# A three-block transformer forward pass with a product-key expert layer: gathering inside the routing, alternating expert tiles, one-hot rows in batches

## The chip, the cores and the metric

The kernel runs on one core of one Trainium2 chip as one program. The metric is the time of one execution on the device, in microseconds (us). The engines are named as in the profile: PE (TensorE, matrix products), PEld (its weight loads), DVE (VectorE), ACT (ScalarE), POOL (GpSimd) and SP (SyncE, which here only issues transfers).

## What is computed

Two blocks of a small model on 512 tokens of width 1024: two layers with feed-forward, attention, mLSTM and RWKV mixing; then one layer with a gated delta rule, an LRU and cross-attention, and last an expert layer and a norm. The change touches only the expert layer:

```
q = (t @ wq).reshape(ntok, 8, 2, 128)            # 8 heads, two half queries
sc = einsum('thpd,hpkd->thpk', q, subkeys)       # 128 keys for each half
s1, i1 = top_k(sc[:, :, 0], 16);  s2, i2 = top_k(sc[:, :, 1], 16)
best, pos = top_k(s1[..., :, None] + s2[..., None, :], 16)
idx = e1 * 128 + e2                              # one of 16384 experts
gate = softmax(best)                             # 128 (expert, gate) pairs for each token
act = gelu(einsum('phkd,pd->phk', u_tab[idx], t)) * gate
out = einsum('phk,phkd->pd', act, v_tab[idx])
```

## The kernel before, in words

Everything lies feature-major in tiles of 128 partitions. A float32 product is made of three products of split operands (high by high, high by low, low by high). A weight tile of 128 x 1024 is therefore loaded into a staging buffer `st` (two of them, 512 KB each), cast by ACT to its high part and subtracted to its low part: `load_w` (lines 173 to 183), with `wh` and `wl` for the tables of u, and lines 1809 to 1812, with `vh` and `vl`, for the tables of v.

The expert layer (`peer`, lines 1557 to 1599) treats the 512 tokens in two ways. For the first 128 tokens (one block) rows are gathered: for each of 128 slots an indirect transfer brings, for every token, the row of its own expert from the u table (`urow`, 512 KB), DVE multiplies and adds it up against the token (line 1767, one number per token into `za`), and eight slots later the row of the v table (`vrow`) is accumulated into `acc` (line 1778). For the other 384 tokens all 16384 experts are computed, 128 tiles of 128 experts: 24 products give z (`peer_z`), then gelu, then the gate of each expert and token (mostly zero), and 18 products add the tile to six accumulators in PSUM (`values`).

The stages in order:

- `peer_route`, lines 1630 to 1723: 16 tiles of query weights; for each tile `lists` (top 16 of 128 keys, for four blocks of tokens, on DVE) and for each of 8 heads `head`: candidates on POOL (`cd`), their top 16 on DVE, comparison on DVE (line 1696), product on POOL (line 1697), sum on DVE (line 1698), softmax. After each head three result tiles of the expert stage are computed early (`early`) and put into DRAM.
- `peer_gates`, lines 1725 to 1747: for each of the 384 tokens three one-hot rows of 128 (lines 1737 to 1739: `o1` the first key, `p1` and `p2` the second key times the gate's high and low part); two products give the token's 128 x 128 gate matrix; ACT copies four tokens at a time into `st` (`gst`), and 32 tokens at a time go to DRAM (`G`, 2 MB). Early result tiles, 30 of them, run between, with the subtraction of `load_w` on POOL (`wl_eng`).
- `peer_experts`, lines 1782 to 1857: 128 tiles. A tile below `NEARLY` (56) fetches its z from DRAM, the others compute it here. Each takes its gates from DRAM (`gt`, 12 pieces for four tiles), makes its activations (`ah`, `al`), loads its v tile, and the products of the tile before it follow.

The gather advances with `gather(n)`: a step of slot s is one DVE product of a u row, one DVE accumulation of a v row, and the issue of the next rows by POOL into the buffers that have come free (three for each table). Before, it begins after the routing: 12 steps in the gates, and the rest with the tiles. The order of instructions on each engine is not the source's: a scheduler places them by dependences and its own estimate, and each engine then works its queue in that order.

Of the kernel before, what the change touches and what calls it, by code (L numbers as in the profile page):

```python
# [21 lines left out]
P = 128  # L22
# [89 lines left out]
class K:  # L112
# [1444 lines left out]
    def peer(self, out):  # L1557
        nc, tc, d = self.nc, self.tc, self.d
        with ExitStack() as ctx:
# [7 lines left out]
            ez = [self.drm.tile([P, TD], F32, tag=f"z{i}", name=f"z{i}", bufs=1) for i in range(NEARLY)]  # L1567
# [7 lines left out]
            self.fin = pool.tile([P, D], F32, name="fin")  # L1575

            def early(n):
                for i in range(self.zi, min(self.zi + n, NEARLY)):
# [4 lines left out]
                    self.zi = i + 1  # L1583

            sl = [pool.tile([P, TD], F32, name=f"slot{i}") for i in range(4)]
# [6 lines left out]
            self.rowp = ctx.enter_context(tc.tile_pool(name="row", bufs=1, reuse_waits="tile"))  # L1592
# [3 lines left out]
            early(NEARLY)  # L1596
            self.wl_eng = nc.vector
# [11 lines left out]
    def token_major(self, yk):  # L1609
# [18 lines left out]
        nc.sync.dma_start(out=self.fin, in_=d["FG"])  # L1628

    def peer_route(self, pool, iota, slots, early, yk):  # L1630
# [27 lines left out]
        def lists(m, q):  # L1658
# [8 lines left out]
            if m % 2:  # L1667
                early(3)

        def head(h):  # L1670
# [39 lines left out]
        nc.vector.scalar_tensor_tensor(self.idx, tok[1][:, 0, :], float(P), tok[0][:, 0, :], op0=ALU.mult, op1=ALU.add)  # L1710
        nc.gpsimd.tensor_copy(out=self.gate0, in_=tok[2][:, 0, :])
        for w in range(3):
# [4 lines left out]
            if w < 2:  # L1717
                nc.scalar.copy(out=slots[w], in_=pf)
            else:
                hi = pool.tile([P, TD], F16, name="hi16")  # L1720
                nc.scalar.activation(hi, pf, AF.Copy, scale=GS)
                nc.vector.scalar_tensor_tensor(slots[3], pf, GS, hi, op0=ALU.mult, op1=ALU.subtract)
                nc.scalar.copy(out=slots[2], in_=hi)

    def peer_gates(self, pool, im, slots, early):

        nc = self.nc
        self.gather_begin()
        for i in range(TD // GT):
            st = pool.tile([P, P, GT], F32, tag="gst", name="gst", bufs=2)  # L1730
            for t0 in range(0, GT, 4):
                pg = self.ps([P, 4, P], "g")
                for j in range(4):
                    t = i * GT + t0 + j
                    o1, p1, p2 = (pool.tile([P, P], F16, tag=n, name=n, bufs=8) for n in ("o1", "p1", "p2"))
                    s = [x[:, t:t + 1] for x in slots]
# [6 lines left out]
                if t0 % 16 == 12:  # L1743
                    early(1)
# [261 lines left out]
```

## Time and profile before

| | us |
|---|---|
| median of 3 runs | 4692.69 (4678.49 to 4698.35) |
| profiled execution | 4696.09 |
| its span | 4694.3 |

| engine | busy us | share of the span | instructions |
|---|---|---|---|
| PE | 4337.1 | 92% | 21867 |
| PEld | 3549.2 | 76% | 21867 |
| DVE | 2823.5 | 60% | 5950 |
| ACT | 1624.7 | 35% | 2583 |
| POOL | 993.5 | 21% | 850 |

The span is from the first to the last instruction on the core. Busy shares are means over stages with different limits, so they say little on one stage. In the rows below, a group of instructions names line, engine, operation, output and inputs (partitions x elements, type) and count; then busy time and the mean of one in ns; then the engine's idle time just before them and what ended most of it. A table of windows gives the busy time of each engine in a stretch of the span, in us from its start.

### The profile page before, as it was taken

The numbers are of one execution on the slowest core, as the hardware profiler recorded it, in microseconds if no ns is written. First come the engines' busy times: TensorE is split into PE (matmuls) and PEld (weight loads), VectorE is DVE, ScalarE is ACT, GpSimd is POOL, SyncE is SP. The second block draws the span as 40 slices with busy tenths as digits, with TensorE's granted clock in tenths as the row PEclk, the third lists the DMA queues.
The fourth block names the chain that finished last, engine by engine and source line by source line (L and its number), as shares of the span: only waits on it lengthen the run. The fifth ranks groups of instructions, "written<-read, shape, count | busy, mean of one in ns | idle before, by whom it ended". The sixth has DMA issues, their size and how long they took to land. (4 is left out here: it accounts for less than half of the span.)

```text
span 4694.3 us, 58390 instructions
## 1 busy us (share of the span) xinstructions
PE 4337.1 (92%) x21867; PEld 3549.2 (76%) x21867; DVE 2823.5 (60%) x5950; ACT 1624.7 (35%) x2583; POOL 993.5 (21%) x850
## 2 busy tenths in 40 slices
PE   8999999999999989999998898998787688888998
PEld 7887787888888867878887677887654466777887
DVE  4435654542654266554427666378899888787334
ACT  3223423322532243233225434332344333322332
POOL 0002110000100031110003321023431666565111
PEclk9999998999999999889998999999997799999999
DMA  3233102323332320122233114333454889898443
GB/s 121 95 96 116 35 19 68 108 94 95 128 109 91 111 89 25 37 72 101 95 110 129 50 37 139 109 138 104 155 183 177 289 313 344 314 331 292 154 149 110
DMA packets 232300, 625.66 MB, mean 133 GB/s; under 512 B 26544, under 2 KB 91184, under 8 KB 227664
## 3 DMA queue, kind: packets, MB, share of 16 engines
q1 hardware_dynamic: 192704, 460.96, 28.8%
q0 software_dynamic: 38736, 159.93, 9.3%
q8 instruction: 171, 2.80, 0.2%
q10 hardware_dynamic: 576, 1.05, 0.1%
q14 instruction: 113, 0.93, 0.1%
HBM read 560.49 MB, written 61.34 MB: 132 GB/s over the span
## 5 line engine op out<-in xcount | busy, mean ns | idle before, releaser
L191 PE MATMUL ps_ps<-xh,wl 128*128 128x512 f32 (+2 forms) x3568 | 1327.3, 373 | 33.0 <-DVE wl L182 32.9
L191 PE MATMUL ps_ps<-xl,wh 128*128 128x512 f32 (+2 forms) x3568 | 1333.9, 374 | 24.1 <-DVE xl L338 23.4
L191 PE MATMUL ps_ps<-xh,wh 128*128 128x512 f32 (+2 forms) x3568 | 1326.8, 373 | 28.3 <-ACT wh L181 15.6
L181 ACT CAST wh<-st 128x1024 fp32r<-128x1024 f32 (+1 forms) x560 | 580.3, 1037 | 1615.7 <-PE ps_ps L191 958.1
L182 DVE TENSOR_TENSOR wl<-st,wh 128x1024 fp32r<-128x1024 f32 (+1 forms) x506 | 613.2, 1213 | 665.5 <-ACT wh L181 664.4
L191 PEld LDWEIGHTS ps_ps<-xh,wl 128*128 128x128 f32 x3568 | 689.5, 193 | 139.7 <-DVE wl L182 40.5
L191 PEld LDWEIGHTS ps_ps<-xl,wh 128*128 128x128 f32 x3568 | 689.5, 193 | 127.3 <-DVE xl L338 34.3
L191 PEld LDWEIGHTS ps_ps<-xh,wh 128*128 128x128 f32 x3568 | 686.4, 193 | 130.1 <-ACT wh L181 17.5
L343 POOL TENSOR_TENSOR y<-y,x 128x256 f32<-128x256 f32 x64 | 54.7, 855 | 1768.8 <-DVE y L342 1534.0
L437 DVE TENSOR_TENSOR gu<-ps_ps,R 128x512 f32<-128x512 f32 x176 | 121.0, 691 | 473.3 <-PE ps_ps L191 473.3
L191 PE MATMUL ps_po<-vh,ah 128*128 128x512 f32 x768 | 318.7, 415 | 66.9 <-ACT ah L1805 65.5
L191 PE MATMUL ps_po<-vl,ah 128*128 128x512 f32 x768 | 319.2, 416 | 45.5 <-DVE vl L1812 45.5
L191 PE MATMUL ps_ps<-mh,wl 128*128 128x512 f32 (+1 forms) x920 | 327.8, 356 | 2.4 <-DVE wl L182 2.4
L191 PE MATMUL ps_po<-vh,al 128*128 128x512 f32 x768 | 318.6, 415 | 11.0 <-DVE al L1806 10.3
L191 PE MATMUL ps_ps<-mh,wh 128*128 128x512 f32 (+1 forms) x920 | 327.4, 356 | 1.2 <-DVE kf L1497 0.9
L191 PE MATMUL ps_ps<-ml,wh 128*128 128x512 f32 (+1 forms) x792 | 289.4, 365 | 0.0
L191 PEld LDWEIGHTS ps_po<-vh,ah 128*128 128x128 f32 x768 | 154.0, 201 | 105.6 <-ACT ah L1805 70.9
L1802 POOL TENSOR_TENSOR z<-z,gt 128x384 f32<-128x384 f32 x128 | 155.6, 1222 | 337.2 <-ACT z L1800 307.3
L191 PE MATMUL ps_g<-p,o 128*128 128x128 f16 x768 | 173.2, 242 | 56.1 <-DVE p L1738 28.1
L191 PEld LDWEIGHTS ps_po<-vl,ah 128*128 128x128 f32 x768 | 153.9, 200 | 87.2 <-DVE vl L1812 56.7
L191 PEld LDWEIGHTS ps_po<-vh,al 128*128 128x128 f32 x768 | 153.8, 200 | 58.2 <-DVE al L1806 26.4
L191 PEld LDWEIGHTS ps_ps<-mh,wl 128*128 128x128 f32 x920 | 174.8, 190 | 26.3 <-DVE wl L182 2.7
(695 smaller groups left out, 6762.7 us busy)
## 6 DMA issues: line engine op xcount, KB each, us to landing
st<-in_pu_dram SPq DMA_DIRECT2D x128, 512.0 KB, 4.4
st<-in_pv_dram SPq DMA_DIRECT2D x128, 512.0 KB, 4.8
st<-in_w1i_dram SPq DMA_DIRECT2D x88, 512.0 KB, 3.5
st<-in_w2i_dram SPq DMA_DIRECT2D x88, 512.0 KB, 3.4
G<-gst POOLq DMA_DIRECT2D x12, 2048.0 KB, 7.7
gt<-G SPq DMA_DIRECT2D x384, 64.0 KB, 5.0
st<-in_wmf_dram SPq DMA_DIRECT2D x44, 512.0 KB, 3.5
xd<-y SPq DMA_DIRECT2D x20, 1024.0 KB, 3.8
```

Of the source, the lines that this page charges most:

```text
L181: nc.scalar.copy(out=wh[:, :n], in_=st[:, :n])
L182: self.wl_eng.tensor_sub(wl[:, :n], st[:, :n], wh[:, :n].bitcast(F32))
L191: i = self.nc.tensor.matmul(out, lhsT=lhsT, rhs=rhs, start=start, stop=stop)
L343: nc.gpsimd.tensor_add(y[k + 1], y[k + 1], self.xin[k + 1][:, c])
L437: nc.vector.tensor_mul(t, psum, R)
L1802: nc.gpsimd.tensor_mul(x3, x3, gts["g"][:, :, i % GK, :])
```

## The change

The gather begins after the first head of the routing, and takes two steps after each head, one after each 16 tokens in the gates (24), and one in three of four turns of the expert tiles (96). Its buffers are fixed: two tiles of the layer's pool and four halves of the buffers that held the layer's input. The early result tiles are no longer the first 56 but two of each four (64), and the turns of four tiles run 0, 2, 1, 3, so early and late tiles alternate. The one-hot rows are built for 16 tokens at once, with tensor-by-tensor instructions of 2048 16-bit elements, in pairs of tokens (the slots are now 16-bit, and the keys are stored twice over). The subtraction of `load_w` in the gates is on DVE again.

```diff
...
-            ez = [self.drm.tile([P, TD], F32, tag=f"z{i}", name=f"z{i}", bufs=1) for i in range(NEARLY)]
+            ez = {i: self.drm.tile([P, TD], F32, tag=f"z{i}", name=f"z{i}", bufs=1) for i in EARLY}
...
+            self.buf = [pool.tile([P, D], F32, name=f"row{i}") for i in range(2)]
...
-            im = pool.tile([P, P], F16, name="im")
-            nc.gpsimd.tensor_copy(out=im, in_=iota)
+            im = pool.tile([P, P, 2], F16, name="im")
+            nc.gpsimd.tensor_copy(out=im, in_=bc(iota.unsqueeze(2), [P, P, 2]))
...
-            self.wl_eng = nc.gpsimd
...
+        h = [self.half(F32, "rows").rearrange("p a b -> p (a b)") for _ in range(2)]
+        self.buf += [h[0][:, :D], h[0][:, D:], h[1][:, :D], h[1][:, D:]]
...
             if m % 2:
                 early(3)
+                self.gather(2)
...
+            nc.vector.scalar_tensor_tensor(self.idx[:, hs], tok[1][:, 0, hs], float(P), tok[0][:, 0, hs], op0=ALU.mult, op1=ALU.add)
+            nc.gpsimd.tensor_copy(out=self.gate0[:, hs], in_=tok[2][:, 0, hs])
+            if h == 0:
+                self.gather_begin()
...
-                    o1, p1, p2 = (pool.tile([P, P], F16, tag=n, name=n, bufs=8) for n in ("o1", "p1", "p2"))
-                    s = [x[:, t:t + 1] for x in slots]
-                    nc.vector.tensor_scalar(o1, im, s[0], None, op0=ALU.is_equal)
-                    nc.vector.tensor_scalar(p1, im, s[1], s[2], op0=ALU.is_equal, op1=ALU.mult)
-                    nc.vector.tensor_scalar(p2, im, s[1], s[3], op0=ALU.is_equal, op1=ALU.mult)
...
+            for t0 in range(0, GT, 2 * B):
+                c = slice(i * GT + t0, i * GT + t0 + 2 * B)
+                o1, p1, p2 = (pool.tile([P, B, P, 2], F16, tag=n, name=n, bufs=2) for n in ("o1", "p1", "p2"))
+                row = lambda x: bc(x[:, c].rearrange("p (a b) -> p a b", b=2).unsqueeze(2), [P, B, P, 2])
+                keys = bc(im.unsqueeze(1), [P, B, P, 2])
+                nc.vector.tensor_tensor(o1, keys, row(slots[0]), op=ALU.is_equal)
+                nc.vector.tensor_tensor(p2, keys, row(slots[1]), op=ALU.is_equal)
+                nc.vector.tensor_mul(p1, p2, row(slots[2]))
+                nc.vector.tensor_mul(p2, p2, row(slots[3]))
+                for q in range(0, B, 2):
...
+                        o, a, b = (x[:, q + j // 2, :, j % 2] for x in (o1, p1, p2))
...
+                    if q == 2:
+                        early(1)
+                early(1 if t0 else 0)
+                self.gather(1)
...
-            t = self.rowp.tile([P, D], F32, tag=w + "row", name=w + "row", bufs=3)
+            t = self.buf[s % 3 + 3 * (w == "v")]
...
-            if i < NEARLY:
+            if i in ez:
...
-            nxt = act(n)
-            due = n // 2 if n < NEARLY else NEARLY // 2 + (n - NEARLY) * 3 // 2
-            self.gather(max(0, due + TD // GT - self.gi))
+            nxt = act(n // 4 * 4 + (0, 2, 1, 3)[n % 4])
+            self.gather(n % 4 != 1)
...
-NEARLY = 56
+EARLY = [i for i in range(P) if i % 4 < 2]
...
```

POOL's queue in the routing of the changed kernel, from the end of the first head (`eq`) to the candidates of the second (`cd`); `row` and `rows` are the gather's buffers, filled from the table of u (`pur`) or of v (`pv`).

```order
L1709 COPY gate_23310<-tok_23335 128x16
L1698 TENSOR_TENSOR eq<-eq,sf 128x1024 x2
L1764 DMA row_23316<-in_pur_dram,idx 128x1024
L1764 DMA row_23317<-in_pur_dram,idx 128x1024
L1764 DMA rows<-in_pur_dram,idx 128x1024
L1764 DMA rows<-in_pv_dram,idx 128x1024
L1764 DMA row_23316<-in_pur_dram,idx 128x1024
L1764 DMA row_23317<-in_pur_dram,idx 128x1024
L1695 CAST sf<-si 128x64
L1764 DMA rows<-in_pv_dram,idx 128x1024 x2
L1678 TENSOR_TENSOR cd<-sv 128x4x8
L1675 COPY cd<-sv 128x4x128
```

Before, `eq` is followed at once by `sf` and the three steps on `cd`; now eight issues of rows stand between, and the second `row_23316` waits for the buffer of the first.

DVE's queue in the gates, before: one token.

```order
L1737 TENSOR_SCALAR o_26202<-im,slot_23308 128x128
L1738 TENSOR_SCALAR p_26203<-im,slot_23309,slot_23310 128x128
L1739 TENSOR_SCALAR p_26204<-im,slot_23309,slot_23311 128x128
L1737 TENSOR_SCALAR o_26212<-im,slot_23308 128x128
L1738 TENSOR_SCALAR p_26213<-im,slot_23309,slot_23310 128x128
```

And of the changed kernel, where this is a batch of 16 tokens:

```order
L1737 TENSOR_TENSOR o_26455<-im,slot_23318 128x2048
L1738 TENSOR_TENSOR p_26457<-im,slot_23319 128x2048
L182 TENSOR_TENSOR wl<-st,wh 128x1024
L1739 TENSOR_TENSOR p_26456<-p_26457,slot_23320 128x2048
L1774 ISA row_23317,za<-row_23317,htok 128x1024
L1774 ISA za 128x1
L1740 TENSOR_TENSOR p_26457<-p_26457,slot_23321 128x2048
L1785 SCALAR_TENSOR_TENSOR acc<-rows,za,acc 128x1024
```

The 48 instructions of 16 tokens became four, and between them stand the subtraction that was POOL's (three for 32 tokens) and a step of the gather for each batch.

DVE's queue in the expert tiles of the changed kernel; `vl` closes a loaded value tile, `wl` a weight tile of a late tile, `z` and `al` are a tile's activations.

```order
L1819 TENSOR_TENSOR vl<-st,vh 128x1024
L1774 ISA row_23316,za<-row_23316,htok 128x1024
L1774 ISA za 128x1
L1785 SCALAR_TENSOR_TENSOR acc<-rows,za,acc 128x1024
L1813 TENSOR_TENSOR al<-z,ah 128x384
L1819 TENSOR_TENSOR vl<-st,vh 128x1024
L1774 ISA row_23317,za<-row_23317,htok 128x1024
L1774 ISA za 128x1
L182 TENSOR_TENSOR wl<-st,wh 128x1024
L1806 TENSOR_TENSOR z<-ps_ps,R 128x384
L1785 SCALAR_TENSOR_TENSOR acc<-rows,za,acc 128x1024
L1774 ISA rows,za<-rows,htok 128x1024
```

Before, early tiles (a `vl` with about one step of the gather) all come first and late ones (`vl` and `wl` with two steps) after them; now each pair of tiles has two `vl`, one `wl` and three steps, and the last step stands after 59 of the 128 tiles, where it stood after 89.

## Rows read from the trace of the kernel before

**Rows 1.** Windows by stage: us, busy PE, PEld, DVE, ACT, POOL, clock, DMA, GB/s

```profile
3095.00:3349.00 254.00, 215.00 (x1090) 193.27 (x1089) 207.00 (x875) 61.55 (x91) 95.23 (x101) 0.95 0.34 114
3349.00:3662.00 313.00, 254.24 (x1476) 155.77 (x1474) 312.85 (x1184) 141.97 (x158) 92.25 (x60) 0.86 0.51 184
3662.00:3686.00 24.00, 0.00 (x0) 0.00 (x0) 19.52 (x24) 7.71 (x15) 21.68 (x13) 0.50 0.88 312
3686.00:4334.00 648.00, 550.78 (x2331) 452.08 (x2332) 535.96 (x643) 201.85 (x299) 415.46 (x311) 0.92 0.90 321
4334.00:4677.00 343.00, 339.05 (x1689) 304.75 (x1688) 136.17 (x175) 116.73 (x159) 41.91 (x41) 1.00 0.43 140
```

**Rows 2.** Groups by line and form, routing, 3095 to 3349 us

```profile
L1698 DVE TENSOR_REDUCE tok<-eq 128x64 f32<-128x1024 f32 x16 | 19.5, 1220 | 27.2 <-POOL eq L1697 27.2
L1696 DVE TENSOR_TENSOR eq<-k,iota 128x1024 f32<-128x1024 f32 x16 | 18.8, 1215 | 0.0
```

**Rows 3.** Groups by line and form, tiles with gather, 3686 to 4334 us

```profile
L1778 DVE SCALAR_TENSOR_TENSOR acc<-vrow,za,acc 128x1024 f32<-128x1024 f32 x119 | 165.4, 1390 | 8.8 <-DMA vrow<-in_pv_dram,idx 8.7
...
L1767 DVE CUSTOM_DVE_ANT_0 urow<-urow,htok 128x1024 f32<-128x1024 f32 x112 | 146.9, 1312 | 1.0 <-DMA urow<-in_pur_dram,idx 1.0
...
L1812 DVE TENSOR_TENSOR vl<-st,vh 128x1024 fp32r<-128x1024 f32 x87 | 108.3, 1245 | 9.2 <-ACT vh L1811 9.1
...
L1811 ACT CAST vh<-st 128x1024 fp32r<-128x1024 f32 x86 | 90.1, 1048 | 120.3 <-DMA st<-in_pv_dram 108.8 <-DVE acc L1778 4.5 <-DVE al L1806 4.1
...
L182 DVE TENSOR_TENSOR wl<-st,wh 128x1024 fp32r<-128x1024 f32 x34 | 41.7, 1226 | 62.4 <-ACT wh L181 62.3
```

**Rows 4.** One tile, urow, 3095 to 3662 us: ns min/median/max

```profile
L1758 POOL DMA_INDIRECT urow<-in_pur_dram,idx x15: 937/997/3129, 3348.5 to 3661.6; - x15
L1767 DVE CUSTOM_DVE_ANT_0 urow<-urow,htok x12: 1206/1214/1225, 3375.6 to 3659.0; 128x1024 f32<-128x1024 f32 x12
...
DMA to landing us min/median/max: 4.9/8.4/11.1
```

**Rows 5.** Timeline of DVE in the gates: start us, us, instruction

```profile
3589.86 0.25 DVE L1737 TENSOR_SCALAR o<-im,slot 128x128 f16<-128x128 f16 x1
...
3590.47 0.25 DVE L1737 TENSOR_SCALAR o<-im,slot 128x128 f16<-128x128 f16 x1
```

**Rows 6.** One tile, im: ns min/median/max, first and last start

```profile
L1737 DVE TENSOR_SCALAR o<-im,slot x384: 235/245/3076, 3349.6 to 3658.3; 128x128 f16<-128x128 f16 x192
```

**Rows 7.** Groups by line and form, gates, 3349 to 3662 us

```profile
L182 POOL TENSOR_TENSOR wl<-st,wh 128x1024 fp32r<-128x1024 f32 x27 | 66.0, 2444 | 109.5 <-ACT wh L181 95.1 <-PE ps_ps L191 11.5 <-PE ps_g L191 2.9
```

**Rows 8.** Groups by line and form, ramp, 3662 to 3686 us

```profile
L1799 DVE TENSOR_TENSOR z<-z,R 128x384 f32<-128x384 f32 x9 | 4.6, 551 | 0.0
```

**Rows 9.** Timeline of PE, tiles alone: first values product, first z product, next values

```profile
4401.79 0.40 PE L191 MATMUL ps_po<-vh,ah 128*128 128x512 f32 x1
...
4405.89 0.34 PE L191 MATMUL ps_ps<-xh,wh 128*128 128x384 f32 x1
...
4410.10 0.40 PE L191 MATMUL ps_po<-vh,ah 128*128 128x512 f32 x1
```

**Rows 10.** Timeline of PE in the gates: gate products, one z product between

```profile
3402.20 0.23 PE L191 MATMUL ps_g<-p,o 128*128 128x128 f16 x1
...
3402.49 0.23 PE L191 MATMUL ps_g<-p,o 128*128 128x128 f16 x1
```

**Rows 11.** DMA issues: count, KB each, median us from issue to landing

```profile
st<-in_pu_dram SPq DMA_DIRECT2D x128, 512.0 KB, 4.4
...
G<-gst POOLq DMA_DIRECT2D x12, 2048.0 KB, 7.7
gt<-G SPq DMA_DIRECT2D x384, 64.0 KB, 5.0
```

**Rows 12.** Windows inside the tiles with gather, columns as in rows 1

```profile
3800.00:3900.00 100.00, 79.18 (x296) 60.96 (x296) 81.86 (x96) 34.22 (x55) 65.71 (x48) 0.88 0.88 310
3900.00:3980.00 80.00, 71.34 (x290) 55.59 (x289) 70.72 (x89) 27.31 (x41) 51.70 (x39) 0.96 0.97 350
```

More of the change, by code (lines that the diff above doesn't have):

```diff
@@ L1575, in peer @@
             self.fin = pool.tile([P, D], F32, name="fin")
+            self.buf = [pool.tile([P, D], F32, name=f"row{i}") for i in range(2)]
             def early(n):
-                for i in range(self.zi, min(self.zi + n, NEARLY)):
+                for i in EARLY[self.zi:self.zi + n]:
                     z = self.peer_z(i)
@@ L1582, in early @@
                     nc.sync.dma_start(out=ez[i], in_=t)
-                    self.zi = i + 1
-            sl = [pool.tile([P, TD], F32, name=f"slot{i}") for i in range(4)]
+                    self.zi += 1
+            sl = [pool.tile([P, TD], F16, name=f"slot{i}") for i in range(4)]
             iota = pool.tile([P, P], F32, name="iota")
             nc.sync.dma_start(out=iota, in_=d["IOTA"])
-            im = pool.tile([P, P], F16, name="im")
-            nc.gpsimd.tensor_copy(out=im, in_=iota)
+            im = pool.tile([P, P, 2], F16, name="im")
+            nc.gpsimd.tensor_copy(out=im, in_=bc(iota.unsqueeze(2), [P, P, 2]))
             with tc.tile_pool(name="pr", bufs=1) as rp:
                 self.peer_route(rp, iota, sl, early, yk)
-            self.rowp = ctx.enter_context(tc.tile_pool(name="row", bufs=1, reuse_waits="tile"))
-            self.wl_eng = nc.gpsimd
             with tc.tile_pool(name="pg", bufs=1, reuse_waits="tile") as gp:
                 self.peer_gates(gp, im, sl, early)
-            early(NEARLY)
-            self.wl_eng = nc.vector
+            early(P)
             with tc.tile_pool(name="px", bufs=1, reuse_waits="tile") as xp:
@@ L1719, in peer_route @@
             else:
[L1720 to L1723, printed above, removed]
+                nc.scalar.activation(slots[2], pf, AF.Copy, scale=GS)
+                nc.vector.scalar_tensor_tensor(slots[3], pf, GS, slots[2], op0=ALU.mult, op1=ALU.subtract)
     def peer_gates(self, pool, im, slots, early):
@@ L1727, in peer_gates @@
         nc = self.nc
[L1728 removed]
+        B = 8
         for i in range(TD // GT):
             st = pool.tile([P, P, GT], F32, tag="gst", name="gst", bufs=2)
[L1731 to L1734, printed above, removed]
[L1735 to L1744 removed]
+            for t0 in range(0, GT, 2 * B):
[8 more added lines that the diff above has]
+                for q in range(0, B, 2):
+                    pg = self.ps([P, 4, P], "g")
+                    for j in range(4):
+                        o, a, b = (x[:, q + j // 2, :, j % 2] for x in (o1, p1, p2))
+                        self.mm(pg[:, j, :], o, a, True, False)
+                        self.mm(pg[:, j, :], o, b, False, True)
+                    t = t0 + 2 * q
+                    nc.scalar.activation(st[:, :, t:t + 4].rearrange("p k t -> p t k"), pg, AF.Copy, scale=1.0 / GS)
+                    if q == 2:
+                        early(1)
+                early(1 if t0 else 0)
+                self.gather(1)
@@ L1745, in peer_gates @@
             nc.gpsimd.dma_start(out=self.gd_[i], in_=st)
-            early(1)
-            self.gather(1)
     def gather_begin(self):
@@ L1842, in peer_experts @@
         self.gather(P + GG)
-        h = [self.half(F32, "xt").rearrange("p a b -> p (a b)") for _ in range(2)]
-        xt = [h[0][:, :D], h[0][:, D:], h[1][:, :D]]
-        sq = h[1][:, D:]
+        xt, sq = self.buf[:NB - 1], self.buf[NB]
         for b in range(NB - 1):
```

5 lines of the change are left out of this document (removed).

## Prediction

> **What bounds the kernel now.** I read the table of windows first, because a change that touches only the last third has to be priced stage by stage. [Rows 1] cut that third at its seams: the routing (254 us), the gates (313), a ramp (24) in which TensorE does nothing, a stage in which expert tiles and the gather share the core (648), and a stage with expert tiles alone (343). The 3095 us ahead are not touched. Three different things bound these stages. In the gates VectorE is busy 312.85 of 313 us, with DMA at half. In the shared stage no engine is full (TensorE 551 of 648), but DMA is at 0.90 and moves 321 GB/s. In the stage of tiles alone TensorE is busy 339 of 343.
>
> Then the groups of instructions by line. The routing has VectorE busy for 207 of 254 us [rows 1], and 27.2 of the idle 47 are the wait of a reduction for GpSimd's product [rows 2]: a chain that goes to and fro between the two. In the shared stage ScalarE's cast, which opens each loaded value tile, stood idle for 108.8 us until the load had come [rows 3]: transfers end last there, not VectorE.
>
> **The change, part by part.** The order of instructions says how many pieces lie in each stage; every duration is from a row.
>
> *Routing, +30.* Of the gather, 17 row products and 9 accumulations now stand on VectorE's queue ahead of the first one-hot row, where none stood. By 1.21 us a product [rows 4] and 1.39 an accumulation [rows 3] that is 33 us; some 2 more for index steps made head by head and for the first row, which lands after about 8.4 us [rows 4] while some ten list steps run. Only one of the 26 stands in the wait of 27.2, so I count 5 us as absorbed by other waits. Bounds: 0, if all falls into the idle 47, and 42, if nothing does and the first row is waited for whole. GpSimd gets some 30 row issues of 1.0 us [rows 4] and has 159 us idle there; ScalarE gets four more table loads and has 192 idle [rows 1]. Both hidden: nothing charged. The wait that the change adds is GpSimd's: a row is issued only when its buffer is free, and the router's casts and products are queued behind it. The cover is three buffers for each table; without it, see the last rival.
>
> *Gates, -49.* A token costs VectorE 0.61 us, start to start [rows 5], so 234 for 384; the rest of the 313 is 16 gather steps and, mostly, waiting: the equality instruction has a median of 245 ns and a maximum of 3076 [rows 6], beside 27 subtractions of 2.44 us on GpSimd [rows 7]. These go to VectorE, and that waiting goes with them. After, 32 tokens take VectorE 8 batches, 3 subtractions (1.23, [rows 3]) and 4 gather steps (1.3). No row shows a batch of 2048 16-bit numbers. By the number of elements, two float32 rows of 384 and 1024 (551 ns, [rows 8]; 1215, [rows 2]) give 1.04 ns an element, so 2.28 us. By bytes, a batch is as long as the row of 1215 ns: 1.22. The 16-bit row of today is the nearest: 128 elements would be 285 ns on the line through those two, and it takes 235 to 245 [rows 6], so it does not pay by elements. I take 1.22 and keep 2.28 as the other end. VectorE then needs 9.8 + 3.7 + 5.2 = 18.7 us for 32 tokens. TensorE needs 3 tiles of 4.21 [rows 9] and 64 gate products of 0.115 (a pair with an expert product repeats every 0.29, [rows 10], of which the latter alone is 4.21/24 = 0.175): 20.0. DMA moves one block of 2 MB, 3 weight tiles and 4 rows of 512 KB [rows 11] and 3 results of 192 KB: 6.4 MB, 19.8 us at 321 GB/s. Three resources within 7% of each other, all with queues in order, wait by turns; I add a tenth: 22 us, times 12 = 264. Bounds: 224 (12 times 18.7) and 325 (12 times 27.1, with 2.28). TensorE has expert tiles to the end of this stage, 36 of them; today they run out, and the granted clock of the stage is 0.86 [rows 1].
>
> *Ramp, 0.* The last block is written and read back (7.7 and 5.0 us, [rows 11]) before the first tile can be used. Four tiles of TensorE work now stand there; they shorten nothing of that path.
>
> *Shared stage, -168.* In VectorE's order the gather, spread over 96 of 128 turns in the source, still runs ahead: from the first cast value tile to the last accumulation there are 58 value tiles, 29 weight tiles, 85 products and 93 accumulations. Today's rows have 87, 34, 112 and 119 [rows 3]. In MB today: 121 tiles and 231 rows of 0.524, and some 140 small ones (gates and early results) of 0.197: 212, which fits [rows 1]'s 321 GB/s over 648 us. After: 87, 178 and 87 of them: 156 MB, 486 us at that rate; by loaded tiles, at 648/121 = 5.36 each, 466. I take 480. Bounds: 446 at the 350 GB/s of the best stretch [rows 12], and 557 at 280, should alternate tiles use DMA worse. For a pair of tiles, early and late, DMA needs 5.3 MB, 16.5 us; VectorE 11.8 for casts, subtractions and gather [rows 3] and some 2.4 for four small steps; TensorE 12.4 (two times 4.10, one of 4.21, [rows 9]). So DMA still ends last, and to alternate is by itself worth nothing: the gain is 53 rows and 34 tiles fewer in this stage.
>
> *Stage of tiles alone, +110.* What leaves the shared stage comes here. Today 39 value and 38 result tiles stand behind the last accumulation, 320 us by [rows 9], and it measures 343, since TensorE runs some tiles behind VectorE. After: 69 and 35, 430, with the same lag 453. TensorE is full here and stays so.
>
> *End and queues, 0.* The final normalisation takes other buffers and the same steps. The sync queue stores and fetches eight more results, 1.6 MB each way, and their bytes are inside the counts above.
>
> Sum: 30 - 49 - 168 + 110 = -77 on the profiled execution's 4696.1 (span 4694.3), which lies 3.4 above the median of the three runs shown. I forecast **4618**.
>
> **Rivals.**
> *All covers hold* (0.15). The router takes most of its 26 steps into its waits (+10), the gates come to 19 us for 32 tokens (228), and the shared stage runs at 350 GB/s (446): 10 - 85 - 202 + 110 = -167, so 4529. For it: DMA held 0.97 for 80 us [rows 12]. Against: the gates need three resources full at once.
> *The batches run one element at a time* (0.17). The slots' operand repeats one pair of 16-bit numbers for each of 128 keys; if that takes the short price away, VectorE needs 27.1 us for 32 tokens, the gates 325: 30 + 12 - 168 + 110 = -16, so 4680. For it: nothing in the trace reads this way. Against: today's 16-bit row. The Trainium skill (Vector Engine (DVE) Microarchitecture Reference, 5.2 Measured stream behaviour on trn2) says that a port keeps its full rate only for runs of two or more adjacent 4-byte words, and gives 1.73 ns a column where one source jumps at each; a pair of 16-bit numbers is one such word, so by it a batch would be an estimated 1.9 us, the gates 290 and the sum some 26 us above mine. No row of this trace can tell.
> *Transfers get worse by turns* (0.08). At 280 GB/s the shared stage is 557: 30 - 49 - 91 + 110 = 0, so 4696, no change. For it: the 100 us ahead of today's best stretch ran at 310 [rows 12]. Against: the rows for each loaded tile hardly move (231/121 = 1.91, then 178/87 = 2.05).
> *The rows hold the router* (0.05; slower). If each of the 26 steps waits as long as a row takes to land (8.4 us, [rows 4]), the routing grows by 218: 218 - 49 - 58 = 111, so 4807. It decides from 4.1 us a step (107/26). For it: VectorE and GpSimd run in order, and the router's lists, candidates and products stand behind. Against: rows are issued two or three ahead, and a head lasts 32 us (254/8).
>
> **How the numbers follow.** The forecast has 0.55 and by itself reaches from 4575 to 4660. Two in ten may stay outside: the slower rival, half of the best case, and edges of the others; so 4520 to 4690. A measurement of this kernel tells about 0.5% from no change, which puts the bounds at 4669 and 4716. Faster: of the forecast 0.54, the best case 0.15, a third of the one-element case 0.06, a little of the worse transfers 0.01: 0.76. Slower: the last rival and edges of two others, 0.08. Same: the rest, 0.16.
>
> **What would show it.** Routing: about 285 us, rows' products between the list steps, no long wait of VectorE for a row. Gates: batches of 1.2 us, 250 to 275 us in all, DMA from 0.5 to over 0.85, clock above 0.95. Shared stage: about 480 us with DMA at 0.9, and ScalarE's casts still idle for loads. Tiles alone: about 450 us, TensorE full. I am wrong if a batch takes 2 us, if the shared stage falls under 450 or stays over 540, or if GpSimd's row issues stand in front of the router's products for long.

## The result, and the profile after

The changed kernel takes **4581.2 us** (median of 4 runs, 4575.1 to 4587.6), beside 4695.5 us for the kernel before in the same session (median of 4). The ratio is 0.9758, 95% interval 0.9721 to 0.9796: 114 us faster. The forecast was 4618, 77 us faster, with a range of 4520 to 4690.

First the table of windows of the changed kernel, cut at the seams of [rows 1]: routing, gates, ramp, shared stage, tiles alone. Columns as there.

```profile
3095.00:3389.00 294.00, 239.20 (x1172) 214.43 (x1171) 242.43 (x953) 76.48 (x110) 143.14 (x136) 0.89 0.47 156
3389.00:3624.00 235.00, 211.37 (x1624) 192.02 (x1623) 204.75 (x205) 141.00 (x169) 85.08 (x58) 0.97 0.84 307
3624.00:3653.00 29.00, 12.69 (x54) 11.19 (x52) 20.31 (x23) 6.89 (x11) 13.57 (x12) 0.70 0.99 355
3653.00:4128.00 475.00, 404.46 (x1712) 334.50 (x1713) 394.23 (x465) 148.02 (x213) 319.76 (x227) 0.90 0.91 324
4128.00:4568.00 440.00, 434.92 (x2092) 380.68 (x2091) 204.73 (x256) 176.80 (x240) 81.64 (x69) 1.00 0.51 166
```

What binds each stage is what bound it before, except in the gates, where VectorE has gone from 312.85 of 313 us to 204.75 of 235 and DMA from 0.51 to 0.84; now nothing is full there, and TensorE is the busiest with 211.37. The stages follow exactly from five events in each trace: the product that makes the gathered tokens' input (`htok`), the first one-hot instruction, the last issue of a gate block, the first value product, the last accumulation of a row.

| us | before | after | difference | forecast |
|---|---|---|---|---|
| routing (`htok` to first one-hot) | 260.4 | 291.1 | +30.7 | +30 |
| gates (to last gate block) | 311.2 | 234.3 | -76.9 | -49 |
| ramp (to first value product) | 25.3 | 29.4 | +4.1 | 0 |
| shared stage (to last accumulation) | 648.3 | 474.7 | -173.6 | -168 |
| tiles alone, and the end | 359.9 | 457.3 | +97.4 | +110 |
| all of it | 1605.1 | 1486.8 | -118.3 | -77 |

The code ahead of `htok` is the same in both and took 9.4 us longer in this execution; with it the spans (4694.3 and 4585.4) differ by 108.9.

Next the groups by line and form in the routing of the changed kernel; the first answers to [rows 2].

```profile
L1699 DVE TENSOR_REDUCE tok<-eq 128x64 f32<-128x1024 f32 x16 | 19.5, 1220 | 28.4 <-POOL eq L1698 28.4
...
L1774 DVE CUSTOM_DVE_ANT_0 row<-row,htok 128x1024 f32<-128x1024 f32 x12 | 14.5, 1210 | 3.5 <-DMA row<-in_pur_dram,idx 3.5
...
L1785 DVE SCALAR_TENSOR_TENSOR acc<-rows,za,acc 128x1024 f32<-128x1024 f32 x9 | 11.6, 1291 | 0.0
...
L1774 DVE CUSTOM_DVE_ANT_0 rows<-rows,htok 128x1024 f32<-128x1024 f32 x5 | 6.2, 1239 | 0.0
```

The wait of the reduction for GpSimd is there as before (27.2, now 28.4): the rows did not fill it. VectorE waited 3.5 us in all for a row. The 17 products and 9 accumulations are those that the prediction counted.

Then the gates, same view: the gate products, the subtraction that came back to VectorE, ScalarE's cast, and a batch.

```profile
L191 PE MATMUL ps_g<-p,o 128*128 128x128 f16 x768 | 57.6, 222 | 10.1 <-DVE p L1739 8.1 <-ACT gst L1748 1.8
...
L182 DVE TENSOR_TENSOR wl<-st,wh 128x1024 fp32r<-128x1024 f32 x35 | 42.8, 1223 | 18.0 <-ACT wh L181 18.0
L181 ACT CAST wh<-st 128x1024 fp32r<-128x1024 f32 x34 | 36.1, 1062 | 82.1 <-DMA st<-in_pu_dram 82.1
...
L1737 DVE TENSOR_TENSOR o<-im,slot 128x2048 f16<-128x2048 f16 x24 | 29.3, 1222 | 0.0
```

And the shared stage, which answers to [rows 3].

```profile
L191 PE MATMUL ps_po<-vh,ah 128*128 128x512 f32 x347 | 153.8, 443 | 75.3 <-ACT ah L1812 75.2
...
L1785 DVE SCALAR_TENSOR_TENSOR acc<-rows,za,acc 128x1024 f32<-128x1024 f32 x89 | 120.5, 1354 | 4.9 <-DMA rows<-in_pv_dram,idx 4.8
...
L1774 DVE CUSTOM_DVE_ANT_0 row<-row,htok 128x1024 f32<-128x1024 f32 x55 | 71.1, 1292 | 0.1
L1818 ACT CAST vh<-st 128x1024 fp32r<-128x1024 f32 x57 | 59.7, 1047 | 35.5 <-DMA st<-in_pv_dram 17.4 <-PE ps_po L191 15.4 <-DMA gt<-G 2.7
L1774 DVE CUSTOM_DVE_ANT_0 rows<-rows,htok 128x1024 f32<-128x1024 f32 x27 | 53.9, 1995 | 0.0
...
L181 ACT CAST wh<-st 128x1024 fp32r<-128x1024 f32 x29 | 30.4, 1050 | 92.1 <-DMA st<-in_pu_dram 92.1
```

55 and 27 products and 89 accumulations where 85 and 93 were counted: the loads and rows of this stage are those of the order, and the rate is 324 GB/s where 321 was used. The cast of value tiles waits 17.4 us for loads, 108.8 in [rows 3]; that wait now stands before the cast of weight tiles, 92.1 us in this stage.

### The profile page after: what moved, and what is told of

Read it like the earlier page. It is cut to its first block, busy times and chain, and to the rows that moved or that the text cites. A ratio compares the mean times of both kernels' runs of the same rounds, so it can differ in the third digit from the quotient of the medians.

```text
span 4585.4 us, 57113 instructions
## 1 busy us (share of the span) xinstructions
PE 4281.3 (93%) x21867; PEld 3575.4 (78%) x21867; DVE 2674.0 (58%) x4931; ACT 1636.7 (36%) x2594; POOL 970.0 (21%) x827
## 5 line engine op out<-in xcount | busy, mean ns | idle before, releaser
L191 PE MATMUL ps_ps<-xh,wh 128*128 128x512 f32 (+2 forms) x3568 | 1325.2, 373 | 31.5 <-ACT wh L181 18.7
L182 DVE TENSOR_TENSOR wl<-st,wh 128x1024 fp32r<-128x1024 f32 (+1 forms) x536 | 650.8, 1215 | 539.2 <-ACT wh L181 538.0
L191 PE MATMUL ps_ps<-ml,wh 128*128 128x512 f32 (+1 forms) x792 | 289.5, 366 | 0.0
L1764 POOL DMA_INDIRECT rows<-in_pv_dram,idx x128 | 197.8, 1546 | 60.6 <-DVE acc L1785 31.3
L191 PEld LDWEIGHTS ps_ps<-mh,wh 128*128 128x128 f32 x920 | 174.5, 190 | 25.8 <-DVE kf L1497 1.2
```

What stands on the lines that cost most here:

```text
L182: self.wl_eng.tensor_sub(wl[:, :n], st[:, :n], wh[:, :n].bitcast(F32))
L191: i = self.nc.tensor.matmul(out, lhsT=lhsT, rhs=rhs, start=start, stop=stop)
L1764: self.nc.gpsimd.indirect_dma_start(out=t, out_offset=None, in_=self.d["pur" if w == "u" else "pvr"], in_offset=bass.IndirectOffsetOnAxis( ...
```

## Experiments

Every time is a median of 4 to 8 runs, with its ratio to the kernel before on the same chip; stages are from the one profiled execution of each, by the five events above. "Experts" is the shared stage and the rest together, from the first value product to the end. The changed kernel has 932.0 us there, the one before 1008.2. The part ahead of `htok`, which is the same in all of them, ends between 3084 and 3106 us in these traces, so a difference of some 20 us between two totals is to be read together with the stages.

| kernel | us | ratio, 95% interval | routing | gates | shared | rest | experts |
|---|---|---|---|---|---|---|---|
| changed | 4581.2 | 0.9758 (0.9721 to 0.9796) | 291.1 | 234.3 | 474.7 | 457.3 | 932.0 |
| rows per token again | 4666.3 | 0.9934 (0.9910 to 0.9958) | 291.0 | 329.0 | 476.8 | 445.7 | 922.5 |
| batches without pairs | 4651.2 | 0.9901 (0.9869 to 0.9932) | 290.8 | 309.5 | 475.0 | 453.7 | 928.7 |
| batches alone | 4621.5 | 0.9830 (0.9801 to 0.9860) | 261.4 | 232.0 | 583.5 | 428.9 | 1012.4 |
| early tiles first | 4606.4 | 0.9812 (0.9779 to 0.9844) | 290.1 | 234.2 | 524.8 | 433.6 | 958.4 |
| gather called after routing | 4545.2 | 0.9680 (0.9660 to 0.9700) | 273.4 | 219.9 | 516.0 | 408.1 | 924.1 |
| gather spread | 4563.7 | 0.9714 (0.9683 to 0.9745) | 289.6 | 239.3 | 889.0 | 26.9 | 915.9 |
| spread, 4 buffers | 4682.0 | 0.9970 (0.9950 to 0.9990) | 289.6 | 235.9 | 993.8 | 36.9 | 1030.7 |
| spread, z fetched | 4655.5 | 0.9904 (0.9868 to 0.9940) | 289.5 | 235.6 | 978.3 | 28.2 | 1006.5 |
| spread, both | 4614.0 | 0.9830 (0.9795 to 0.9864) | 290.2 | 235.3 | 932.4 | 37.0 | 969.4 |
| spread, two turns | 4527.9 | 0.9629 (0.9600 to 0.9658) | 291.1 | 233.1 | 853.3 | 26.9 | 880.2 |
| spread, two turns, z fetched | 4590.9 | 0.9762 (0.9746 to 0.9779) | 289.4 | 235.1 | 912.0 | 26.9 | 938.9 |
| two turns, gather called after routing | **4512.0** | 0.9601 (0.9579 to 0.9623) | 273.7 | 213.9 | 875.0 | 28.2 | 903.2 |

### The gates

Theory: the batches are what shortens the gates, and a batch takes 1.22 us because its slot operand steps through a pair of 16-bit numbers. Rival: the other parts of the change do as much.

**Rows per token again**, all else as changed.

```diff
-                nc.vector.tensor_tensor(o1, keys, row(slots[0]), op=ALU.is_equal)
...
+                    nc.vector.tensor_scalar(o1, im, s[0], None, op0=ALU.is_equal)
+                    nc.vector.tensor_scalar(p1, im, s[1], s[2], op0=ALU.is_equal, op1=ALU.mult)
+                    nc.vector.tensor_scalar(p2, im, s[1], s[3], op0=ALU.is_equal, op1=ALU.mult)
```

> The changed kernel with one part undone: the one-hot rows are again three instructions for each token; the subtraction of the weight tiles stays on VectorE, the gather stays where the change put it. Theory (VectorE's instructions made the gates long): 32 tokens cost 19.5 + 3.7 + 4.9 = 28.1 us on VectorE, so the gates go from 234 to about 335 us and the whole from 4581 to about 4680, ratio to before 0.995 to 1.0. Rival (it was the wait for GpSimd's subtractions that made them long, and the batches add little): gates 240 to 265 us, the whole 4585 to 4610.

**Batches without pairs**: the same 96 instructions of 2048 elements, with the keys innermost, so that the slot operand repeats one 16-bit number 128 times.

```diff
-                row = lambda x: bc(x[:, c].rearrange("p (a b) -> p a b", b=2).unsqueeze(2), [P, B, P, 2])
+                row = lambda x: bc(x[:, c].unsqueeze(2), [P, 2 * B, P])
```

> The changed kernel with batches of 16 tokens, but tokens not in pairs: the keys run innermost, and the slot's operand repeats one 16-bit number for 128 elements. Theory (the pair in the innermost place is what lets the batch run at the price by bytes): a batch takes about 2.28 us in place of 1.22, VectorE needs 27 us for 32 tokens, the gates come to 320 us and the whole to about 4670. Rival (16 bits suffice): 1.22 us, gates 234, 4575 to 4590.

**Batches alone**: the kernel before with the batches; beside them only the buffers of the v rows move, to make room.

```diff
+                nc.vector.tensor_tensor(o1, keys, row(slots[0]), op=ALU.is_equal)
+                nc.vector.tensor_tensor(p2, keys, row(slots[1]), op=ALU.is_equal)
+                nc.vector.tensor_mul(p1, p2, row(slots[2]))
+                nc.vector.tensor_mul(p2, p2, row(slots[3]))
...
-            t = self.rowp.tile([P, D], F32, tag=w + "row", name=w + "row", bufs=3)
+            t = self.rowp.tile([P, D], F32, tag=w + "row", name=w + "row", bufs=3) if w == "u" else self.vbuf[s % 3]
```

> The kernel before with the one-hot rows in batches of 16 tokens and nothing else of the change: early tiles stay the first 56, the gather begins in the gates, the subtraction of load_w in the gates stays on POOL (only the rows of v move to the buffers that held the layer's input, since the batches need the room). Theory: the batches alone pay the gain in the gates, and a shorter gates stage is worth its whole length because nothing after it depends on the other parts. VectorE then has 96 x 1.22 = 117 us of one-hots and some 65 us of rows in this stage, TensorE 27 tiles x 4.2 + 58 us of gate products = 171 us, so about 205 to 240 us in place of 311, and a total of 4590 to 4630, ratio 0.977 to 0.986: more than three quarters of the whole gain of 114. Rival: the parts need each other (the batches without the gather begun in the routing leave the same rows for the experts, and POOL's subtraction holds the early tiles): the gates stay over 270 us and the total over 4655.

The windows of the gates of the three, in this order, then the batch without pairs and the row products of batches alone by line:

```profile
3385.00:3714.00 329.00, 262.19 (x1588) 218.73 (x1587) 326.07 (x1259) 145.39 (x167) 57.28 (x55) 0.82 0.61 215
```

```profile
3380.00:3689.00 309.00, 226.08 (x1591) 207.95 (x1590) 304.77 (x203) 140.19 (x168) 110.66 (x57) 0.86 0.68 231
```

```profile
3357.00:3590.00 233.00, 187.39 (x1467) 178.89 (x1465) 227.05 (x181) 134.94 (x162) 172.12 (x90) 0.91 0.85 311
```

```profile
L1737 DVE TENSOR_TENSOR o<-im,slot 128x2048 f16<-128x2048 f16 x24 | 54.8, 2282 | 0.0
```

```profile
L1772 DVE CUSTOM_DVE_ANT_0 urow<-urow,htok 128x1024 f32<-128x1024 f32 x27 | 36.1, 1335 | 1.0 <-DMA urow<-in_pur_dram,idx 1.0
```

With rows per token, or with batches of 2.28 us, VectorE is full again (326 of 329, 305 of 309) and the gates are 95 and 75 us longer; the experts hardly move (922.5, 928.7). So the batch's price carries the stage, and about nine tenths of it reach the total: 85 of 95 us, 70 of 75. Batches alone give 78 us, about 70% of the gain where over three quarters were expected. They do not need the rest of the change: the scheduler put 27 row products into their gates, where 12 stood before, and GpSimd's subtractions, which stay in that run, did not hold them. The theories hold in kind; the gates of the first two are 6 and 10 us under what was expected, the totals 14 and 19.

### The order of the early tiles

The prediction has it that alternating tiles is by itself worth nothing.

```diff
-            nxt = act(n // 4 * 4 + (0, 2, 1, 3)[n % 4])
+            nxt = act(n)
...
-EARLY = [i for i in range(P) if i % 4 < 2]
+EARLY = list(range(64))
```

> The changed kernel with the alternation undone: the 64 early tiles are the first 64 and come first. In VectorE's order the gather then ends at tile 80 of 128 and not at 59. Theory (bytes at 324 GB/s): the shared stage holds 172 MB, about 530 us (475 with alternation), the stage after it about 420 (457 with the end): +20 to +40, the whole 4600 to 4620. Rival 1 (the order of early and late is worth nothing): 4570 to 4592. Rival 2 (alternation is what made the gain): over 4650.

4606, inside what was expected: **alternating is worth 25 us** by the medians, 26 in the experts. The two intervals of the ratio touch, but no run of one kernel lies among the other's. The windows of the shared stage and of the tiles alone:

```profile
3646.00:4170.00 524.00, 436.32 (x1779) 350.73 (x1779) 435.89 (x513) 172.81 (x263) 328.71 (x248) 0.91 0.90 321
4170.00:4589.00 419.00, 414.50 (x2060) 371.54 (x2059) 168.31 (x212) 141.40 (x192) 49.67 (x49) 1.00 0.44 139
```

DMA moves the same 321 GB/s. But with early tiles first, TensorE is left without work for 524 - 436 = 88 us of the shared stage; alternating, for 475 - 404 = 71: 17 of the 25 us. The shared stage also holds more, 168 MB where alternating holds 154 (rate times length, from these rows and those of the changed kernel). The prediction looked at DMA, which ends last in either order, and not at how much of TensorE's work is done meanwhile.

### The gather in the routing

With the rows in it the routing is 30.7 us longer. Do they bring as much later?

```diff
-                self.gather(2)
...
-            if h == 0:
-                self.gather_begin()
...
+        self.gather_begin()
         B = 8
...
-            self.gather(n % 4 != 1)
+            self.gather(n % 8 != 1)
```

> The changed kernel with the gather begun in the gates again: no row is fetched or worked on in the routing, and the experts take seven steps in eight turns in place of three in four. Theory (the prediction's: a step moved out of the full shared stage pays its transfer there and costs what it holds up in the routing): the routing goes from 291 back to some 260 us; 16 steps or 16 MB more in the shared stage are 16 MB / 0.32 = 50 us, and that stage ends some 8 tiles later, which takes as many from the stage of tiles alone; the sum is nearly nothing, total 4565 to 4600. Rival: the routing's 30 us are the price of POOL's queue, and what is bought with them is hidden anyway: 4550 to 4560. Other rival: the rows in the routing are what lets the shared stage end early, and without them 4610 or more.

4545: 36 us **faster** than the change, and better than the expectations. They were also wrong in one point: the scheduler still put rows into the routing, where nothing but its own estimate asked for them, 11 products and 2 accumulations in place of 17 and 9.

```profile
L1772 DVE CUSTOM_DVE_ANT_0 row<-row,htok 128x1024 f32<-128x1024 f32 x8 | 9.7, 1211 | 0.0
...
L1772 DVE CUSTOM_DVE_ANT_0 rows<-rows,htok 128x1024 f32<-128x1024 f32 x3 | 3.6, 1208 | 0.0
...
L1783 DVE SCALAR_TENSOR_TENSOR acc<-rows,za,acc 128x1024 f32<-128x1024 f32 x2 | 2.5, 1253 | 0.0
```

The routing is 17.7 shorter for 13 instructions less, 1.4 each, and the gates 14.4. The rows come back in the shared stage, which is 41.3 us longer, and the stage after it is 49.2 shorter. So as it stands in this change, a row taken in the routing costs its full time there and buys nothing: the experts take 932 us with the rows moved ahead and 924 without, though the routing and the gates then hold 11 products and 10 accumulations fewer. What a variant with no row at all in the routing would do wasn't tried.

### The gather spread over all tiles

In the shared stage TensorE is short of work, in the next one DMA. Theory: let the gather steps keep pace with the tiles (each step behind the subtraction `vl` of its turn, on VectorE), and neither is.

```diff
+                self.behind(i, self.after)
...
-            nc.vector.tensor_sub(vl, st, vh.bitcast(F32))
+            self.after = nc.vector.tensor_sub(vl, st, vh.bitcast(F32))
```

> The changed kernel with one addition: in the expert tiles each step of the gather stands behind the subtraction of its own turn's value tile on VectorE's queue (an order, no wait), so the 96 steps are spread over all 128 tiles as the source has them, and don't run ahead. Theory (DMA ends last in the shared stage and TensorE in the one after it, since the gather is bunched): a pair of tiles then needs 3.7 MB, 11.5 us at 324 GB/s, under TensorE's 12.4, so the whole expert part runs near TensorE: 64 pairs in 800 to 840 us where it now takes 915; the whole 4480 to 4520. Rival (loads are late at any mean load, for their latency with two staging buffers): the casts' idle time for loads stays and the whole stays at 4560 to 4590.

4563.7: 17 us of the 61 to 101 that the theory expected, 16 of them in the experts. That lies in the rival's 4560 to 4590, but its reason, late loads, is not what TensorE waits for in the rows. The rows of the spread kernel from 3700 to 4400 us: the window, TensorE's waits, ScalarE's cast.

```profile
3700.00:4400.00 700.00, 642.25 (x2927) 536.68 (x2926) 475.23 (x572) 248.34 (x351) 322.05 (x245) 0.98 0.77 261
```

```profile
L191 PE MATMUL ps_po<-vh,ah 128*128 128x512 f32 x588 | 240.3, 409 | 27.4 <-ACT ah L1815 27.4
L191 PE MATMUL ps_po<-vh,al 128*128 128x512 f32 x588 | 240.2, 409 | 30.4 <-DVE al L1816 30.4
...
L1821 ACT CAST vh<-st 128x1024 fp32r<-128x1024 f32 x98 | 102.2, 1043 | 125.4 <-PE ps_po L191 77.8 <-DMA st<-in_pv_dram 36.0 <-DMA gt<-G 11.4
```

DMA has room (0.77), and TensorE stops 58 us for its activations `ah` and `al`. ScalarE meanwhile waits for TensorE (77.8 us, for a buffer of `vh`), and the cast to `ah` is queued behind. Five runs took the suspects apart.

**Four buffers** (`vh`, `vl`, `ah`, `al`):

```diff
-            vh = pool.tile([P, 1024], F32R, tag="vh", name="vh", bufs=3)
+            vh = pool.tile([P, 1024], F32R, tag="vh", name="vh", bufs=4)
```

> The spread gather (4563.7 before this) with four in place of three buffers for each of vh, vl, ah and al. In the spread kernel ACT stood idle for 97 us before the cast to vh because TensorE still read the buffer. Theory A (buffers of the v tile bind): some 30 us or more go, 4520 to 4540. Theory B (the in-order wait of VectorE for the early tile's z from DRAM binds, 109 us of idle time before that instruction): nothing, 4555 to 4570.

**z fetched** ahead, into buffers of its own; `turns` is the list of tiles in their order:

```diff
+            fetch(n + 4)
...
+            zt[turns[n]] = pool.tile([P, TD], F32, tag="ze", name="ze", bufs=3)
+            nc.sync.dma_start(out=zt[turns[n]], in_=ez[turns[n]])
```

> The spread gather with the early tile's z fetched four turns ahead into three buffers of its own; buffers of vh, vl, ah, al as they were. Theory B: VectorE no longer stands before the z of the early tile, the subtraction to al behind it comes in time, TensorE loses its stops and the half clock that follows them: 4490 to 4535. Theory A: ACT's wait for vh stays, 4550 to 4570.

**Both:**

> Both at once: z fetched four turns ahead and four buffers for vh, vl, ah, al. If either chain alone held the turn, this equals the better of the two; if they take turns, it is better than both: 4460 to 4520, the floor being TensorE's own 12.4 us for each of 64 pairs, some 110 us below the spread kernel.

All three missed: they are slower than the spread kernel by 118, 92 and 50 us, and no theory had that. Both together are better than either alone, but worse than leaving both out. The same rows with four buffers:

```profile
3700.00:4400.00 700.00, 596.63 (x2567) 494.24 (x2565) 428.64 (x502) 214.29 (x309) 277.52 (x216) 0.92 0.69 230
```

```profile
L191 PE MATMUL ps_po<-vh,ah 128*128 128x512 f32 x512 | 220.5, 431 | 54.2 <-ACT ah L1815 53.9
L191 PE MATMUL ps_po<-vh,al 128*128 128x512 f32 x511 | 220.1, 438 | 46.2 <-DVE al L1816 46.1
...
L1821 ACT CAST vh<-st 128x1024 fp32r<-128x1024 f32 x86 | 89.9, 1045 | 154.2 <-PE ps_po L191 132.7 <-DMA st<-in_pv_dram 16.8 <-PE ps_ps L191 4.6
```

The wait of the cast for TensorE has grown, with a buffer more. In the order of instructions the scheduler used the fourth buffer to move the cast to `vh` up by one tile in ScalarE's queue, ahead of the previous tile's `ah`: in the spread kernel 125 of the 128 casts to `ah` have two casts to `vh` more than casts to `ah` ahead of them, and with four buffers 92 have three more. So it waits for the same products as before, and more stands behind it. That gave a new theory: a loop (TensorE's products free `vh`, ScalarE casts into it, the `ah` behind that cast lets TensorE go on), to be widened on TensorE's side.

**Two turns** between activations and products, with four buffers:

```diff
-            nxt = act(n // 4 * 4 + (0, 2, 1, 3)[n % 4])
+            ops.append(act(n // 4 * 4 + (0, 2, 1, 3)[n % 4]))
...
-            if ops:
+            if len(ops) > 2:
+                old = ops.pop(0)
```

> The spread gather with the value products two turns behind their activations in place of one, and four buffers for vh, vl, ah, al; the order on VectorE and ACT is that of the spread kernel, only TensorE's value products stand one tile later. Theory (TensorE stops for a loop: its products free a vh buffer, ACT casts into it, and the cast to ah that TensorE needs stands behind it on ACT; the loop spans two turns): over three turns the loop has room, the stops go, and with them the stretches at half clock behind them; a pair of tiles takes 12.5 to 13.2 us in place of 14.1: 4480 to 4515. Rival (the transfers hold the turn, at 260 GB/s as they are issued): no change, 4555 to 4575.

4527.9. The order on ScalarE and VectorE is nearly that of the spread kernel (124 of 128 casts to `ah` have two more casts to `vh` ahead), and the loop is gone: the cast waits for TensorE no more, TensorE for `ah` and `al` 7 us in place of 58, and the clock is at 1.00.

```profile
3700.00:4400.00 700.00, 655.62 (x3086) 563.79 (x3086) 489.14 (x600) 261.40 (x370) 340.71 (x259) 1.00 0.80 275
```

```profile
L191 PE MATMUL ps_po<-vh,al 128*128 128x512 f32 x613 | 240.0, 391 | 7.4 <-DVE al L1816 7.3
L191 PE MATMUL ps_po<-vh,ah 128*128 128x512 f32 x614 | 239.6, 390 | 0.0
...
L191 PE MATMUL ps_ps<-xh,wl 128*128 128x384 f32 x416 | 146.8, 353 | 37.8 <-DVE wl L182 37.6
...
L1821 ACT CAST vh<-st 128x1024 fp32r<-128x1024 f32 x103 | 107.4, 1042 | 82.6 <-DMA st<-in_pv_dram 82.6
```

The mechanism holds; the size was too hopeful (4480 to 4515), for a new wait took part of it: 37.8 us for `wl`. The casts to `vh` wait longer for loads here than in the spread kernel, 82.6 us and 36.0, so late loads did not hold that one. Two turns with three buffers were not tried.

**Two turns and z fetched:**

> As the spread kernel with two turns between, and the early tile's z fetched four turns ahead. Theory of the loop: as the one without the fetch, within 15 us of it, 4480 to 4515, since a wait that no longer reaches TensorE costs nothing. Rival (VectorE's wait for z bounds the turn by itself): over 20 us better than it. Second rival (the other order on the engines is what made the fetch slower, by 92 us with one turn between): slower than it by 30 us or more.

4590.9, the second rival: the fetch costs 63 us with two turns as it cost 92 with one. Here TensorE waits for `wl` alone, 71.9 us in the same 700, and the fetched order puts `al` of the late tile on VectorE straight behind `wl`, where it stands idle 114 us for `ah`.

```profile
L191 PE MATMUL ps_ps<-xh,wl 128*128 128x384 f32 x379 | 143.0, 377 | 71.9 <-DVE wl L182 71.9
...
L1815 DVE TENSOR_TENSOR al<-z,ah 128x384 fp32r<-128x384 f32 x47 | 54.2, 1153 | 114.3 <-ACT ah L1814 114.3
```

That this is the whole price was not tried apart.

### The two findings together

Two turns, spread, and the gather's calls moved behind the routing.

> The spread gather with two turns between activations and products, and the gather's calls in the gates and with the tiles alone, as in the run that moved them there: the scheduler is free to begin a few rows in the routing, in gaps of its own choice (it put 11 of them there in that run, in place of 18), and the experts take seven steps in eight turns. Theory (the two findings are in different stages, so they add: 20 us from a shorter routing, 14 from the gates with fewer rows, and the expert turns are held by TensorE, which has no more to do with more rows): 30 us or so below the run with two turns, 4485 to 4505, the fastest of all. Rival (the spread turn is bound by its transfers, 275 GB/s and the row steps on VectorE and POOL, so that each row moved back costs its 3 us): no gain, 4520 to 4545.

**4512.0**, the lowest median of all: 69 us under the changed kernel and 187 under the one before. Of two turns alone it is not clear: those runs go from 4510.3 to 4535.0, these from 4510.0 to 4514.3. The median lies between the ranges of theory and rival, and the stages share it between them: routing and gates are 17.4 and 19.2 shorter than with two turns alone, about as expected, and the experts take back 23.0, which the theory had at nothing.

## Why the prediction was right, and where it was off

**What binds each stage** was right: the exchange between VectorE and GpSimd in the routing, DMA in the shared stage (0.91, 324 GB/s), TensorE in the tiles alone (434.92 of 440).

**Routing, +30**: measured +30.7. VectorE's row work does not fit into the waits, as argued; the wait for GpSimd stayed at 28.4 and GpSimd's row issues held nothing for long (3.5 us of waiting for a row). The rival that the rows hold the router fell.

**Gates, -49**: measured -76.9, and this term is most of the error of 37. The batch was right, 1222 ns for 1.22 us, and so "the batches run one element at a time" fell. By the Trainium skill's rule (Vector Engine (DVE) Microarchitecture Reference, 5.2), as the prediction applied it, a batch would have taken an estimated 1.9 us; the measurement does not agree, 1.22 with pairs and 2.28 without. Mis-sized was above all TensorE's piece. "64 gate products of 0.115" cost 57.6 us / 768 = 0.075 each: the 0.115 came from a pair of which one was an expert product, and here most run in blocks of 14 and 16. With 0.075 TensorE has 17.4 us of work for 32 tokens and not 20.0, and it measures 211.37 / 12 = 17.6. DMA's 19.8 was too much as well: 307 GB/s over 235 us are 72 MB, 6.0 for 32 tokens and not 6.4, since the last 2 MB block leaves behind the stage and 34 weight tiles stood in it where 36 were counted. VectorE has 17.1 for the 18.7 counted. "I add a tenth", for which the prediction had no row, then held: none of the three is full (0.90, 0.87 and 0.84), so they do wait for each other, and 17.6 and a tenth are 19.4, beside a measured 234.3 / 12 = 19.5. The sign given for this stage, 250 to 275 us, was missed.

**Ramp, 0**: +4.1. DMA is at 0.99 there where it was at 0.88; what holds it was not tried.

**Shared stage, -168**: measured -173.6. The counts from the order and the rate of [rows 1] gave it. The sentence that "to alternate is by itself worth nothing" failed: 25 us by experiment. The term came out right all the same, since the rows counted in it were those of the alternating order.

**Tiles alone, +110**: measured +97.4, with the end in it. The tiles are those counted (69 value tiles, 34 result tiles for 35), 430 us. The lag of 23 us that was taken over from before is the term that was off: it came to some 10, 440 us in the window.

**"Transfers get worse by turns"** fell: 324 GB/s. "All covers hold" was half right: the gates came close to its 228, the routing and the rate did not.

One thing the sum did not show. Shared stage and tiles alone are one account: what leaves the first mostly comes back in the second, and the total is TensorE's own work (an estimate from [rows 9]: 128 x 4.10 + 64 x 4.21 = 794 us for the changed kernel, 828 before with 72 late tiles) and what it stands still or runs slow, the end of the kernel included: 138 us after, 180 before, 86 with two turns. Of the 76 us that the experts gained, 34 are by this estimate the eight tiles more that are made early.

## What to carry to other kernels

Where two stages follow each other with different limits, count what the engine that fills the second one does in the first: moving work between them pays only as far as that engine stands still less, and work moved into a third stage whose waits do not take it up (here rows into the routing) is paid in full. A buffer more does not widen a loop if the scheduler spends it on moving the waiting instruction further up; look at where that instruction stands in its queue, and widen the loop on the consumer's side. For a short operand that is broadcast, let the innermost step run through two adjacent 16-bit numbers: 1.22 us in place of 2.28 for 2048 elements.

## What the runs showed of the hardware

**A short stop of TensorE costs more than itself.** In the spread kernel it waited 2.24 us for `al`, and the next products came at 0.43 us apart where they had come at 0.23. TensorE's rows there, then the windows before the stop, behind it, and after that (busy PE, clock, DMA, GB/s): behind the stop the granted clock is 0.50, the lower of its two levels (1.2 GHz), and then 1.00 again (2.4 GHz). The seven products from 4010.58 to 4013.42 took 2.84 us where at 0.23 they would have taken 1.6.

```profile
4005.88 0.39 PE L191 MATMUL ps_po<-vl,ah 128*128 128x512 f32 x1
4006.11 0.39 PE L191 MATMUL ps_po<-vh,al 128*128 128x512 f32 x1
...
4007.35 0.40 PE L191 MATMUL ps_po<-vl,ah 128*128 128x512 f32 x1
4009.99 0.80 PE L191 MATMUL ps_po<-vh,al 128*128 128x512 f32 x1 [2.24 <-DVE al L1816]
4010.58 0.63 PE L191 MATMUL ps_po<-vh,ah 128*128 128x512 f32 x1
4011.01 0.63 PE L191 MATMUL ps_po<-vl,ah 128*128 128x512 f32 x1
...
4013.42 0.39 PE L191 MATMUL ps_po<-vl,ah 128*128 128x512 f32 x1
```

```profile
4002.20:4007.00 4.80, 4.29 (x20) 1.00 0.97 349
4010.60:4013.10 2.50, 2.50 (x7) 0.50 0.45 138
4013.40:4020.00 6.60, 6.60 (x36) 1.00 0.54 174
```

**VectorE's row products stretch beside GpSimd's.** In the shared stage of the changed kernel the products on `rows` take 1995 ns, those on `row` 1292, the same instruction on equal sizes. Timeline of VectorE, then of GpSimd:

```profile
3909.84 2.01 DVE L1774 CUSTOM_DVE_ANT_0 rows<-rows,htok 128x1024 f32<-128x1024 f32 x1
...
3916.66 1.22 DVE L1774 CUSTOM_DVE_ANT_0 row<-row,htok 128x1024 f32<-128x1024 f32 x1
...
3917.80 2.03 DVE L1785 SCALAR_TENSOR_TENSOR acc<-rows,za,acc 128x1024 f32<-128x1024 f32 x1
```

```profile
3909.43 1.34 POOL L1809 TENSOR_TENSOR z<-z,gt 128x384 f32<-128x384 f32 x1 [1.49 <-ACT z L1807]
...
3917.58 1.18 POOL L1809 TENSOR_TENSOR z<-z,gt 128x384 f32<-128x384 f32 x1
```

Both long instructions began while GpSimd's product ran, and ended 1.08 and 1.07 us after its end: nearly as if they had started only then. The buffer's name is not the reason. Over the whole execution, 27 of the 42 products on `rows` began while GpSimd computed (its issues of rows not counted), with a median of 2.02 us, and 13 met no such instruction, with one of 1.22; of the 86 on `row` only 8 began so, with 2.02, and 68 met none, with 1.22. The Trainium skill (SBUF — State Buffer, SBUF: two separate sides) says that VectorE, reading two operands in SBUF, and GpSimd, reading SBUF too, lock each other out of a shared port for a whole instruction; these rows agree. In the spread kernel, where the two seldom fall together, the same products have a median of 1218 ns.
